# Dilated q, k and v in seven products: one encoder layer on one Trainium2 core

## The chip, the cores and the metric

The program runs on one core of a Trainium2 chip. Five engines work side by side: TensorE (PE in the profile; PEld is its weight load), VectorE (DVE), ScalarE (ACT), GpSimd (POOL) and SyncE (SP), which issues most DMAs. The metric is the time of one execution on the device, in microseconds; shorter is better. Of the kernel before, three executions took 1961.05, 1961.09 and 1961.69 us; their median, 1961.09 us, is the time to compare with.

## The reference

One layer of a bidirectional encoder on 256 tokens of width 4096, all in float32:

```python
h = rms_norm(x, g_mix)
proj = h @ w_in                       # 4096 x 9792
c_q, c_kv, k_rope, gate_a, q_b, k_b, v_b, gate_b = split(proj)   # 1024|512|64|2048|2048|2048|2048|2048
q_a  = rms_norm(c_q) @ w_uq           # 1024 x 3072, rotary on 64 of each head's 192
kv   = rms_norm(c_kv) @ w_ukv         # 512 x 4096
y_a  = rms_norm(mla_attention(...)) * silu(gate_a)               # group A: 16 heads of 128
y_b  = rms_norm(dilated_mixture_attention(q_b, k_b, v_b)) * silu(gate_b)   # group B: 16 heads of 128
x = x + concat([y_a, y_b]) @ w_out    # 4096 x 4096
x = x + (p @ w_ple) * sigmoid(rms_norm(x, g_ple) @ w_ple_gate)   # 256 x 4096 and 4096 x 4096
out = rms_norm(x, g_final)
```

The dilated attention of group B merges three patterns (window, dilation) by their softmax denominators; with 256 tokens that is one softmax over the 256 x 256 scores of a head, with a distance penalty and a table of how many patterns hold each pair. `g_ple` is scaled by 3.513, nothing else is changed in the inputs.

## The kernel before

**The products.** Every operand of a large product is split into two float32r halves, `hi` (a rounded copy, made by ACT, L115) and `lo` (the rest, a subtraction on DVE, L116), and a product is three matmuls: `hi*hi`, `lo*hi`, `hi*lo` (`mm`, L130 to L135). A weight is fetched by SP into one of 4 `raw` buffers of 512 KB, converted to `hi` and `lo` in a ring of 3 buffers (`wp`; some stages add more slots), and used by PE as the streamed operand, 512 columns at a time; the tokens' 128x128 blocks are the stationary operand.

**Two forms of a stage.** A `Chunk` computes 512 columns for both halves of the 256 tokens in two PSUM banks: a step takes two row blocks of 128 weights, and so 12 matmuls of 128x512. A `Block` (L691) computes 1024 columns in eight PSUM banks. Its row blocks go in pairs, by one of two recipes. In a plain pair two steps of 12 matmuls make eight products of 128 tokens x 128 rows x 512 columns. In a fast pair (`fast_steps`, L734) four steps make seven such products (M1 to M7), from four differences of weights that DVE forms (L742) and from four sums of token blocks that are made once for the whole stage (`add_sums`, L772); the seven are added up in PSUM over the pairs, and combined when the last pair is through: `..._mid` behind the last fast pair, `..._done` behind the last step of the block. The string in `mix` gives the order, C a plain pair and S a fast one.

**The order.** `steps` is the list of all steps in the order of PE: the four chunks of 400 columns with the latents, gate A's four chunks with the products of `w_uq` and `w_ukv` between them, then for each group of four dilated heads a chunk of q, of k and of v (`done_d`, L589), gate B's four chunks, three `Block`s and two chunks of `w_out`, three `Block`s and the rest of `w_ple_gate`. After each step `advance` (L240) is called once (a tick): it lets every small task go one `yield` further. Tasks are spawned by the `done` of a chunk (into `urgent`), or, for heads of attention, put into `waiting` and started one by one, two ticks apart, at most five at a time. So the engines' queues, which each execute in the order of the program, hold the conversions for the next steps and the pieces of small tasks in turn. A step's conversion stands two steps ahead of its use with the ring of 3, and five steps ahead where a stage has a longer ring (L1312).

**Attention.** A head (`attend`, L387) takes ten ticks: PE turns q and k (L393, L394), both are split (L397), PE makes the scores `s`, DVE and ACT the softmax (L420 to L433 in a dilated head), PE turns the weights (L440), they are split into `pt` (L443), PE multiplies with v into `o`, ACT copies it out (L449) and squares it (L451), POOL adds the squares (L453). The MLA heads run beside gate A's second chunk; the dilated heads of a group of four run beside the chunks of the next group, the last four beside gate B's first chunk. v comes split from `done_d`.

**Gates.** `done_gate` (L534) applies SiLU to a gate chunk, scales it, turns it on PE (L556), multiplies it with the attention output (L561), and splits the product into `yT`, the token side of `w_out`. The four chunks go in a chain, each behind the `yT` of the one before. `y_sums` makes the sums for the fast pairs of `w_out`.

**Banks.** PSUM has eight banks of 128x512, `m0` to `m3`, `s`, `o`, `t0`, `t1`. A stage's first matmul into a bank waits until the former contents have been read. In `w_out` the last chunk uses `o` and `m1` (L1128), and the first `Block` of `w_ple_gate` starts in `m1` (`TAGS`, L699).

## Time and profile before

The profiled execution took 1961.72 us, with a span of 1960.0 us on the core; the rest lies around the span.

| engine | busy, us | share of the span |
|---|---|---|
| PE (matmul) | 1941.6 | 99% |
| PEld (weight load) | 1658.0 | 85% |
| DVE | 1277.4 | 65% |
| ACT | 1011.1 | 52% |
| POOL | 71.2 | 4% |

HBM traffic is 188 GB/s over the span. A row of the profile's groups names line, engine, operation, out<-in with shapes, the count, then after a bar the busy time and the mean duration of one in ns, then the idle time before it and who ended it. A row of a table by stretches gives, after the bounds in us, the length, then for PE, PEld, DVE, ACT and POOL the busy time with the number of instructions that overlap the stretch, then PE's granted clock (1.00 is full), the share of the DMA engines and GB/s. In a timeline, a row is start, duration, engine, line, operation, with the idle time before it in brackets.

By stages, PE: the latents and gate A to about 441 us, the twelve chunks of dilated q, k and v with twelve of the sixteen dilated heads to about 1050, gate B to about 1226, `w_out` to about 1584, `w_ple_gate` to the end.

### The profile page before, as it was taken

What the parts mean: (1) busy time and instruction counts of PE and PEld (TensorE: products, weight loads), DVE (VectorE), ACT (ScalarE), POOL (GpSimd) and SP (SyncE); (2) the same over time, 40 slices, a digit from 0 to 9 for tenths busy, and PEclk for the clock granted to TensorE, in tenths of its full rate; (3) what the DMA queues carried; (4) which work ended last, traced back from release to release, by engine and by line L of the source; (5) the groups of instructions that cost most, each with busy time, mean ns of one, the idle gap of its engine ahead of it and who ended that gap; (6) DMA issues with size and microseconds to landing.
All of it is one profiled execution on the core that took longest, in us unless ns stands there. A gap on an engine that the chain in (4) does not pass through costs nothing.

```text
span 1960.0 us, 25219 instructions
## 1 busy us (share of the span) xinstructions
PE 1941.6 (99%) x9434; PEld 1658.0 (85%) x9434; DVE 1277.4 (65%) x1685; ACT 1011.1 (52%) x1375; POOL 71.2 (4%) x124
## 2 busy tenths in 40 slices
PE   9999999999999999999999999999999999999997
PEld 8998899988888888888888888888888878888887
DVE  7645566664564644645645555888867588888765
ACT  6544555554454544544544544555545455656543
POOL 1001111100000000000000100000000000000000
PEclk9999999999999999999999999999999999999999
DMA  7666544546656566566565666665656556566655
GB/s 251 189 185 198 167 145 141 155 151 204 184 182 194 161 192 190 157 193 186 167 194 179 219 187 200 198 208 194 204 185 208 189 188 213 195 223 197 227 186 177
DMA packets 175146, 370.56 MB, mean 189 GB/s; under 512 B 11924, under 2 KB 45808, under 8 KB 174768
## 3 DMA queue, kind: packets, MB, share of 16 engines
q1 hardware_dynamic: 173104, 361.80, 58.8%
q0 software_dynamic: 1920, 7.15, 1.0%
q8 instruction: 74, 1.21, 0.2%
q14 instruction: 48, 0.39, 0.1%
HBM read 364.72 MB, written 4.19 MB: 188 GB/s over the span
## 4 chain that ended last, share of the span: by engine, by line
PE 98%; DVE 1%; ACT 0%; DMA 0%; issue 0%; SPq 0%; DVEq 0%; ACTq 0%
PE m L133 26%; PE m L134 26%; PE m L135 26%; PE s L134 2%; PE s L135 2%; PE s L133 2%; PE t L133 2%; PE t L134 2%; PE t L135 2%; PE o L134 2%; PE o L135 2%; PE o L133 2%; PE t L440 1%; PE t L393 0%; DMA raw<-in_w_in_dram 0%; PE t L394 0%
## 5 line engine op out<-in xcount | busy, mean ns | idle before, releaser
L116 DVE TENSOR_TENSOR lo<-raw,hi 128x1024 fp32r<-128x1024 f32 (+4 forms) x596 | 695.2, 1171 | 534.9 <-ACT hi L115 534.4
L115 ACT ACTIVATE hi<-raw 128x1024 fp32r<-128x1024 f32 (+4 forms) x596 | 599.9, 1011 | 623.5 <-PE m L135 477.2
L133 PE MATMUL m<-hi,Ah 128*128 128x512 f32 (+2 forms) x1730 | 661.0, 382 | 2.7 <-ACT junk L672 1.8
L134 PE MATMUL m<-lo,Ah 128*128 128x512 f32 (+2 forms) x1730 | 655.0, 379 | 0.2 <-DVE lo L116 0.2
L135 PE MATMUL m<-hi,Al 128*128 128x512 f32 (+2 forms) x1727 | 653.4, 378 | 0.0
L133 PEld LDWEIGHTS m<-hi,Ah 128*128 128x128 f32 x1730 | 325.5, 188 | 55.8 <-issue 2.2
L135 PEld LDWEIGHTS m<-hi,Al 128*128 128x128 f32 x1727 | 324.7, 188 | 55.7 <-DVE Al L127 0.2
L134 PEld LDWEIGHTS m<-lo,Ah 128*128 128x128 f32 x1730 | 325.5, 188 | 52.8 <-DVE lo L116 0.5
L133 PE MATMUL m<-hi,B 128*128 128x512 f32 (+1 forms) x398 | 151.7, 381 | 0.0
L135 PE MATMUL m<-hi,B 128*128 128x512 f32 (+1 forms) x398 | 148.3, 373 | 0.0
L134 PE MATMUL m<-lo,B 128*128 128x512 f32 (+1 forms) x398 | 148.1, 372 | 0.0
L135 PEld LDWEIGHTS m<-hi,B 128*128 128x128 f32 x398 | 74.8, 188 | 10.8
L134 PEld LDWEIGHTS m<-lo,B 128*128 128x128 f32 x398 | 75.0, 188 | 9.7
L133 PEld LDWEIGHTS m<-hi,B 128*128 128x128 f32 x398 | 74.9, 188 | 9.8
L116 DVE TENSOR_TENSOR T<-t,T 128x512 fp32r<-128x512 f32 (+1 forms) x65 | 44.4, 683 | 39.4 <-ACT T L115 39.1
L453 POOL TENSOR_TENSOR acc<-acc,junk 128x256 f32<-128x256 f32 x30 | 29.3, 978 | 798.2 <-ACT junk L451 798.2
L116 DVE TENSOR_TENSOR B<-raw,B 128x1024 fp32r<-128x1024 f32 (+1 forms) x35 | 38.0, 1100 | 17.8 <-ACT B L115 17.8
L115 ACT ACTIVATE B<-raw 128x1024 fp32r<-128x1024 f32 (+1 forms) x35 | 32.8, 957 | 22.5 <-PE m L135 10.0
L133 PE MATMUL m<-B,Ah 128*128 128x512 f32 (+1 forms) x107 | 40.1, 374 | 0.0
L134 PE MATMUL m<-B,Ah 128*128 128x512 f32 (+1 forms) x107 | 40.0, 374 | 0.0
L135 PE MATMUL m<-B,Al 128*128 128x512 f32 (+1 forms) x107 | 40.0, 374 | 0.0
L115 ACT ACTIVATE T<-t 128x512 fp32r<-128x512 f32 (+1 forms) x65 | 38.3, 590 | 0.0
(625 smaller groups left out, 2427.6 us busy)
## 6 DMA issues: line engine op xcount, KB each, us to landing
raw<-in_w_in_dram SPq DMA_DIRECT2D x320, 512.0 KB, 3.4
raw<-in_w_out_dram SPq DMA_DIRECT2D x128, 512.0 KB, 4.5
raw<-in_w_ple_gate_dram SPq DMA_DIRECT2D x128, 512.0 KB, 4.6
raw<-in_w_in_dram SPq DMA_DIRECT2D x63, 400.0 KB, 3.3
raw<-in_w_uq_dram SPq DMA_DIRECT2D x32, 384.0 KB, 3.4
raw<-in_w_ukv_dram SPq DMA_DIRECT2D x16, 512.0 KB, 3.7
T<-in_x_dram POOLq DMA_DIRECT2D x8, 512.0 KB, 7.2
out_dram<-T SPq DMA_DIRECT2D x16, 256.0 KB, 2.6
```

Of the source, the lines that this page charges most:

```text
L115: nc.scalar.activation(hi, src, AF.Copy)
L116: nc.vector.tensor_tensor(lo, src, plain(hi), op=ALU.subtract)
L133: nc.tensor.matmul(ps, ah, bh, start=start, stop=False)
L134: nc.tensor.matmul(ps, ah, bl, start=False, stop=False)
L135: nc.tensor.matmul(ps, al, bh, start=False, stop=stop)
L440: nc.tensor.transpose(tp[:, k, t * P:(t + 1) * P], e[:, t, k * P:(k + 1) * P], ident)
L453: nc.gpsimd.tensor_tensor(acc, acc, sq, op=ALU.add)
```

## The change

Dilated q, k and v are no longer twelve chunks of 512 columns with four heads at a time, but six `Block`s of 1024 columns, in the order q, k, v of heads 0 to 7 and then of heads 8 to 15. Five of them have six fast pairs of sixteen and the last has four: 34 of 96 pairs. The sums of the token blocks for six pairs are made by a new task `x_sums`, beside gate A's last chunk; it waits for the MLA heads' statistics, which are now taken 32 steps earlier. `d_mid` and `d_done` combine the products and scale them by the tokens' norm.

All 16 dilated heads then wait until the last block is through and run beside the four chunks of gate B, one started two or three ticks behind the former. v is kept in float32, so a head splits its own part of v (`vs`) beside `pt`; its output is written over its q. The MLA half of the gated output stays in its place in float32 (`ya`), and `split_ya` splits it when the buffers of v and k are free. The chain of the gates follows the turned chunk now, not the split one.

`Block` gets its banks from outside. Consecutive blocks of q, k, v and of `w_out` alternate between two assignments, `EVEN` and `ODD`: a block begins with plain products (M2, X, M3, M4) in the four banks that the former block had for M1, M5, M6 and M7, the products that only fast pairs use and that `..._mid` reads out. The first block of `w_out` has four fast pairs instead of five. The last two chunks of `w_out` use `m2`, `m3` and `m0`, `m1`, and the blocks of `w_ple_gate` start in `m2`, `m3`, `s`, `o`.

```diff
     def advance():
         ticks[0] += 1
-        if waiting and len(running) < 5 and ticks[0] - ticks[1] >= 2 and waiting[0][0] <= flags:
+        if waiting and len(running) < 5 and ticks[0] - ticks[1] >= waiting[0][2] and waiting[0][0] <= flags:
             running.append(waiting.pop(0)[1])
             ticks[1] = ticks[0]
...
         pt = slot(f"T{2 + h % 2}", [2, NT, S], F32R)
         split(pt[:, 0], pt[:, 1], tp)
+        if dil:
+            vs = slot(("Q0", "T6")[h % 2], [2, NT, HD], F32R)
+            split(vs[:, 0], vs[:, 1], v)
+            v = lambda kt: (vs[:, 0, kt], vs[:, 1, kt])
         yield
         o = bank("o", [S])
         for k in range(NT):
-        nc.scalar.activation(y, o, AF.Copy)
+        nc.scalar.activation(y, by_token(o) if dil else o, AF.Copy)
...
+            u = slot(U_TAGS[dil][c], [NT, 512])
             for t in range(NT):
                 nc.scalar.activation(u[:, t], ps[t], AF.Tanh, scale=rxh[:, t:t + 1])
                 nc.vector.scalar_tensor_tensor(u[:, t], u[:, t], 1.0, ps[t], op0=ALU.add, op1=ALU.mult)
                 yield
-            while ("ry", dil) not in flags or (c and ("yT", dil, c - 1) not in flags):
+            while ("ry", dil) not in flags or (c and ("turned", dil, c - 1) not in flags):
                 yield
             yield
...
+                if b:
+                    flags.add(("turned", dil, c))
                 yield
...
-                    kt = 2 * b + k
-                    g = G["ob" if dil else "oa"][:, 4 * c + kt:4 * c + kt + 1]
-                    nc.vector.scalar_tensor_tensor(w[:, k], y[c // 2][:, 4 * (c % 2) + kt], g, tp[:, k],
+                    h = 4 * c + 2 * b + k
+                    g = G["ob" if dil else "oa"][:, h:h + 1]
+                    y = yb_rows(h) if dil else by_token(y_rows(ya, h))
+                    nc.vector.scalar_tensor_tensor(by_token(w[:, k]) if dil else y, y, g, by_token(tp[:, k]),
                                                    op0=ALU.mult, op1=ALU.mult)
+            if not dil:
+                flags.add(("gated", c))
+                return
+            while (("yT", 0, 3) if c == 0 else ("yT", 1, 1)) not in flags and c != 1:
+                yield
...
+    def split_ya():
+
+        for c, tag in enumerate(("B0", "B1", "B2", "B4")):
+            while not all(("head", 1, h) in flags for h in range(HEADS if c else HEADS // 2)):
+                yield
+            both = slot(tag, [2, 4, S], F32R)
+            yT[c] = [both[:, 0], both[:, 1]]
+            for b in range(2):
+                at = slice(4 * (c % 2) + 2 * b, 4 * (c % 2) + 2 * b + 2)
+                split(*(q[:, 2 * b:2 * b + 2] for q in yT[c]), ya[c // 2][:, at])
+                yield
+            flags.add(("yT", 0, c))
...
+    D_TAGS = {("q", 0): ("B5",), ("k", 0): ("B7a", "B7b"), ("v", 0): ("B0",),
+              ("q", 1): ("B6",), ("k", 1): ("B4",), ("v", 1): ("B1",)}
...
+    def d_mid(key, blk):
+        def task():
...
+            ps = blk.ps
+            sc = [(rxq if key[0] == "q" else rx)[:, t:t + 1] for t in range(NT)]
+
+            def add(h, t, m, old):
+                nc.vector.scalar_tensor_tensor(d[h][:, t], ps[m], sc[t], old, op0=ALU.mult, op1=ALU.add)
+
+            for t in range(NT):
+                nc.scalar.activation(d[0][:, t], ps["M1"], AF.Copy, scale=sc[t])
+            for t in range(NT):
+                add(1, t, "M6", d[0][:, t])
+            add(0, 1, "M7", d[1][:, 1])
+            add(1, 0, "M5", d[1][:, 0])
+            add(1, 1, "M5", d[0][:, 1])
+            flags.add(("mid", key))
+            yield
+        return task
...
+    def d_done(key, blk):
+        def task():
+            d = D[key]
+            sc = [(rxq if key[0] == "q" else rx)[:, t:t + 1] for t in range(NT)]
+            for m, t, h in (("M2", 0, 0), ("X", 1, 1), ("M3", 0, 1), ("M4", 1, 0)):
+                nc.vector.scalar_tensor_tensor(d[h][:, t], blk.ps[m], sc[t], d[h][:, t], op0=ALU.mult, op1=ALU.add)
+            if key == ("v", 1):
+                E["t"] = slot("T4", [2, NT, S])
+                for h in range(HEADS):
+                    waiting.append((set(), attend(
+                        h, lambda t, h=h: d_cols("q", h)[:, t], lambda t, h=h: d_cols("k", h)[:, t], None,
+                        d_cols("v", h), yb_rows(h), True), 2 + h % 2))
+                spawn(y_stats(1))
+                spawn(split_ya())
             yield
         return task
...
-        TAGS = dict(M1="m0", M2="m1", M3="m2", M4="m3", M5="s", M6="o", M7="t0", X="t1")
+        NAMES = "M2", "X", "M3", "M4", "M1", "M5", "M6", "M7"
+
+        def __init__(self, w, lhs, sums, name, order, needs, tags, tmp, ring):
             self.w, self.lhs, self.sums, self.name, self.needs, self.tmp = w, lhs, sums, name, needs, tmp
-            self.ring = ring
+            self.ring, self.tags = ring, dict(zip(self.NAMES, tags))
...
+                if isinstance(self.tmp, tuple):
+                    T.extend(slot(b, [2, Q]) for b in self.tmp)
+                else:
+                    both = slot(self.tmp, [4, Q])
+                    T.extend((both[:, :2], both[:, 2:]))
...
+        while not all(("yT", 0, c) in flags for c in range(FAST_O // 2)):
+            yield
+        yield from add_sums(FAST_O, lambda j: [q[:, 2 * (j % 2):2 * (j % 2) + 2] for q in yT[j // 2]], zy_dst, "Al1",
+                            "y_sums", y_s)
...
-    WIDE_PLE = {(0, 0): "m0", (0, 1): "s", (1, 0): "o", (1, 1): "t0"}
+    WIDE_PLE = {(0, 0): "m0", (0, 1): "m1", (1, 0): "t0", (1, 1): "t1"}
...
-    for g in range(4):
-        for i, off in enumerate((OFF_Q, OFF_K, OFF_V)):
-            add(from_x(off + 512 * g, 512, done_d(i, g)))
+    EVEN, ODD = ("m0", "m1", "s", "o", "m2", "m3", "t0", "t1"), ("m2", "m3", "t0", "t1", "m0", "m1", "s", "o")
+    LAST = "m2", "m3", "s", "o", "m0", "m1", "t0", "t1"
...
+    def x_sums():
+        while ("ry", 0) not in flags:
+            yield
+        yield from add_sums(6, lambda j: [q[:, 2 * (j % 4):2 * (j % 4) + 2] for q in xT[j // 4]],
+                            lambda j: slot(z_tags[j], [2, 4, P], F32R), "B0", "x_sums", x_s)
+
+    hook(64 + 16 + 64, lambda: spawn(y_stats(0)))
+    hook(64 + 16 + 64 + 12, lambda: spawn(x_sums()))
+    gated_rings = {("T4", "T7"): ("mid", ("k", 1)), "Al1": ("y_sums", FAST_O - 1)}
+    for n, key in enumerate((key, i) for i in range(2) for key in "qkv"):
+        off = {"q": OFF_Q, "k": OFF_K, "v": OFF_V}[key[0]] + 1024 * key[1]
+        order = mix("CCCCSCSCSCSCSCSC" if n < 5 else "CCCCCSCCSCCSCCSC")
+        ring = (["B4", "B6"], ["B4", "B6"], ["B4", "B6"], ["B4", "B1"], ["B1"], [("T4", "T7")])[n]
+        blk = Block(w_in[:, off:off + 1024], lhs_x, x_s, "x_sums", order, lambda kt: (), (EVEN, ODD)[n % 2],
+                    "B1" if n < 3 else ("T5", "T6"), WP + ring)
+        lay(blk, order, d_mid(key, blk), d_done(key, blk))
+    for c in range(4):
+        if c == 3:
+            hook(len(steps) + 8, lambda: spawn(y_sums()))
+        ch = from_x(OFF_GB + 512 * c, 512, done_gate(1, c))
+        ch.banks = M[c % 2]
+        add(ch)
+
     for k in range(WIDE_O):
-        hook(len(steps), only("t0", "m0"))
+        hook(len(steps), only(*(("t0", "t1"), ("m0", "m1"), ("m2", "m3"))[k]))
         for h in range(2):
             hook(len(steps) + 4 + h, lambda c=2 * k + h: load_res(c))
-        order = mix(("CCCCCSCSCSCSCSCC", "CCCSCSCSCSCSCSCC", "CCCSCCSCCSCCSCCC")[k])
+        order = mix(("CCCCCCSCSCSCSCCC", "CCCSCSCSCSCSCSCC", "CCCSCCSCCSCCSCCC")[k])
         blk = Block(w_out[:, 1024 * k:1024 * (k + 1)], lhs_y, y_s, "y_sums", order, lambda kt: need_y(kt // 2),
-                    "Al2" if k < 2 else "Al1", WP + (["Ah2", "Al1"] if k < 2 else [("T6", "T7")]))
+                    (EVEN, ODD)[k % 2], "Al2" if k < 2 else "Al1", WP + (["Ah2", "Al1"] if k < 2 else [("B7b", "T7")]))
         lay(blk, order, out_mid(k, blk), out_done(k, blk))
...
-        add(Chunk(cols(w_out, 512 * c, 512), 32, 512, lhs_y, ("m0", "s") if c == 6 else ("o", "m1"), done_o(c), need_y))
+        add(Chunk(cols(w_out, 512 * c, 512), 32, 512, lhs_y, ("m2", "m3") if c == 6 else ("m0", "m1"), done_o(c), need_y))
...
-                    lambda kt: [("x1T", kt // 4)], "B4", WP + ["B5", "B6"])
+                    lambda kt: [("x1T", kt // 4)], LAST, "B6", WP + ["B4", "B5"])
-    tail_banks = {6: (("m0", "s"), ("o", "t0")), 7: (("m1", "m3"), ("m2", "t1")), 8: (("m0", "s"), ("o", "t0"))}
+    tail_banks = {6: (("m0", "m1"), ("t0", "t1")), 7: (("m2", "o"), ("s", "m3")), 8: (("m0", "m1"), ("t0", "t1"))}
...
-        if i == 64 + 16 + 64 + 32:
-            spawn(y_stats(0))
-        if i == 64 + 16 + 64 + 32 + 192:
-            spawn(y_stats(1))
```

More of the change, by code (lines that the diff above doesn't have):

```diff
@@ L383, in encoder_layer @@
     ya = [None, None]
-    yb = [None, None]
     E = {}
@@ L532, in y_stats @@
         flags.add(("ry", dil))
+    U_TAGS = ("B7a", "B7b", "T5", "T6"), ("T7", "B7a", "B7b", "T4")
     def done_gate(dil, c):
         def task(ps):
-            y = (yb if dil else ya)
-            if not dil and c < 2:
-                u = slot(("B7a", "B7b")[c], [NT, 512])
-            else:
-                u = slot(f"T{5 + c % 2}", [NT, 512])
+            u = slot(U_TAGS[dil][c], [NT, 512])
             for t in range(NT):
@@ L960, in load_p @@
         split(pt[:, 0], pt[:, 1], tp, 0.5)
+        P4[0, 0] = slot("Q0", [Q])
+        P4[0, 1] = junk
         flags.add("pT")
@@ L1127, in encoder_layer @@
             hook(len(steps) + 11, lambda: spawn(load_p()))
[L1128 to L1129 removed]
+        add(Chunk(cols(w_out, 512 * c, 512), 32, 512, lhs_y, ("m2", "m3") if c == 6 else ("m0", "m1"), done_o(c), need_y))
+    kept = [("B1",), ("B4",), ("B5",), ("B6",), ("B7a", "T6")]
     stay = []
@@ L1234, in tiles @@
         n = at[0] % len(ring)
-        if ring[n] == "Al1" and ("y_sums", FAST_O - 1) not in flags:
+        if ring[n] in gated_rings and gated_rings[ring[n]] not in flags:
             n = 0
```

107 lines of the change are left out of this document (34 added, 73 removed).

## The prediction

> **What bounds the kernel now.** I read first the page's busy shares and its 40 slices, then the chain that ended last, then a table of busy time by stretches, then who PE waited for.
>
> ```profile
> span 1960.0 us, 25219 instructions
> ...
> PE 1941.6 (99%) x9434; PEld 1658.0 (85%) x9434; DVE 1277.4 (65%) x1685; ACT 1011.1 (52%) x1375; POOL 71.2 (4%) x124
> ...
> PEclk9999999999999999999999999999999999999999
> ...
> PE 98%; DVE 1%; ACT 0%; DMA 0%; issue 0%; SPq 0%; DVEq 0%; ACTq 0%
> ```
>
> PE is busy for 99% of the span and is 98% of the chain, at full clock in every slice. A busy PE can still be a waiting one, so the pace has to be read from the starts of matmuls. The next rows are from the timeline at the end of `w_out`.
>
> ```profile
> 1581.91 0.39 PE L133 MATMUL m<-hi,B7a 128*128 128x512 f32 x1
> ...
> 1583.72 0.39 PE L135 MATMUL m<-hi,B7b 128*128 128x512 f32 x1
> 1585.91 0.47 PE L133 MATMUL m<-hi,Ah 128*128 128x512 f32 x1 [1.80 <-ACT junk L672]
> ...
> 1582.75 1.21 DVE L116 TENSOR_TENSOR lo<-raw,hi 128x1024 fp32r<-128x1024 f32 x1
> 1583.88 0.68 DVE L116 TENSOR_TENSOR B<-B,B 128x512 fp32r<-128x512 f32 x1
> 1584.48 0.68 DVE L671 TENSOR_TENSOR T<-o,T 128x512 f32<-128x512 f32 x1
> 1585.08 0.68 DVE L671 TENSOR_TENSOR T<-m,T 128x512 f32<-128x512 f32 x1
> ...
> 1587.66 2.36 DVE L116 TENSOR_TENSOR B<-raw,B 128x1024 fp32r<-128x1024 f32 x2 [1.90 <-ACT B L115]
> ```
>
> From 1581.91 to 1583.72 there are eight pitches: 0.226 us for a matmul of 128x512, though each is shown 0.39 long. Then PE starts nothing for 2.19 us, 1.96 more than a pitch: the first product of the `w_ple_gate` block wants bank m1, and the last reader of m1's old contents is the second L671, which stands behind DVE's backlog and ends at 1585.76. The waits view knows one other stop of any size behind the start, (`o L133`, at 400 us), in a part that the change doesn't touch.
>
> ```profile
> PE m L133 <- ACT junk L672: 1.8, 1, 1.8
> ...
> PE o L133 <- ACT T L115: 0.7, 1, 0.7
> ```
>
> So the time is PE's instruction count times its pitch, as long as DVE and ACT keep up. How near they are to not keeping up is seen in stretches: plain chunks, the densest dilated attention, and the first `w_out` block, with fast pairs.
>
> ```profile
> core 0: us, PE busy (x) PEld busy (x) DVE busy (x) ACT busy (x) POOL busy (x), PEclk, DMA share, GB/s
> 690.00:735.00 45.00, 45.00 (x200) 37.29 (x199) 21.59 (x18) 17.74 (x18) 0.00 (x0) 1.00 0.64 197
> 654.00:668.00 14.00, 14.00 (x76) 12.10 (x75) 10.17 (x20) 9.29 (x18) 0.00 (x0) 1.00 0.49 151
> 1226.00:1313.00 87.00, 87.00 (x389) 72.04 (x388) 75.36 (x100) 50.23 (x56) 0.00 (x0) 1.00 0.60 199
> 1568.00:1617.00 49.00, 47.20 (x214) 38.75 (x213) 43.22 (x75) 27.43 (x36) 0.32 (x1) 1.00 0.58 188
> ```
>
> DVE is half idle under plain chunks, at 73% in dense attention, and at 87% in the `w_out` block, where PE still lost nothing. The last row is the stretch with the stop: 1.80 us less PE, and a granted clock of 1.00.
>
> **The change, part by part.**
>
> *Matmuls.* A fast pair has seven products where a plain one has eight, a product is three matmuls: 34 x 3 = 102 fewer. The first `w_out` block goes from five fast pairs to four: 3 more. In the order of instructions the built programs have 6906 and 6807 matmuls of 128x512, and equal numbers of all others. 99 x 0.226 = 22.4 us come off PE, the engine that bounds.
>
> *The stop at 1583.72.* The chunk before the `w_ple_gate` block now fills m0 and m1, and the block starts in m2, m3, s, o; m2 and m3 were read out a chunk earlier. The stop has no cause left: -1.96 us. Next late would be the third step's `B` conversion: its DVE half (1587.66, the first of two) is done by 1588.9, and without the stop PE gets there after two steps of 12, 1583.95 + 5.4 = 1589.4. It fits by 0.6, so I take -1.9; the ends are -1.9 and 0.
>
> *DVE and ACT in the six blocks.* Durations are from the groups kept apart by shape; L119 and L127 stand for operations out of PSUM, L778 for the short ones of the sums.
>
> ```profile
> L116 DVE TENSOR_TENSOR lo<-raw,hi 128x1024 fp32r<-128x1024 f32 x477 | 585.5, 1232 | 463.0 <-ACT hi L115 462.7
> L115 ACT ACTIVATE hi<-raw 128x1024 fp32r<-128x1024 f32 x477 | 503.1, 1060 | 546.1 <-PE m L135 416.2 <-PE s L135 57.1 <-issue 34.8
> L742 DVE TENSOR_TENSOR B<-raw,B 128x512 f32<-128x512 f32 x36 | 24.8, 689 | 0.6
> L116 DVE TENSOR_TENSOR T<-t,T 128x512 fp32r<-128x512 f32 x64 | 44.0, 688 | 39.4 <-ACT T L115 39.1
> L119 DVE SCALAR_TENSOR_TENSOR B<-m,st,B 128x512 fp32r<-128x512 f32 x8 | 5.7, 751 | 1.8 <-ACT B L118 1.8
> L127 DVE SCALAR_TENSOR_TENSOR Al<-t,gT,Ah 128x256 fp32r<-128x256 f32 x52 | 22.7, 478 | 2.3 <-ACT Ah L125 2.3
> L778 DVE TENSOR_TENSOR Al<-Al 128x128 f32<-128x128 f32 x9 | 2.3, 288 | 0.2
> ```
>
> A fast pair costs DVE 4 x 0.689 + 0.688 + 3 x 1.232 = 7.1 us, a plain pair 2 x 1.232 = 2.5. A block of ten plain and six fast pairs: 25 + 43 + nine read-outs x 0.751 = 6.8, together 74 us, against PE's (16 x 24 - 18) x 0.226 = 82.7: 90%, by means that overlap (1582.75 + 1.21 ends behind the next start, 1583.88). The `w_out` block carries 87% as measured, with the same recipe and without loss to PE; where S and C alternate, 7.1 + 2.5 = 9.6 stand under 4.7 + 5.4 = 10.1. ACT has 20 x 1.06 and 6 x 3.5 x 1.06, 43 of 82.7. I take 0 and keep 0 to +10 (0.3 us for each of 34 pairs).
>
> *Handing on the banks.* A new wait: a block's first products want the banks that `d_mid` of the former reads, one plain pair after the last fast one. The nearest case before is `wide_mid`, whose banks are wanted by the `w_ple` step, also one plain pair later.
>
> ```profile
> 1658.16 0.39 PE L135 MATMUL o<-hi,B7a 128*128 128x512 f32 x1
> ...
> 1659.06 0.68 DVE L922 TENSOR_TENSOR B<-B,o 128x512 f32<-128x512 f32 x1
> ...
> 1661.10 0.69 DVE L922 TENSOR_TENSOR B<-B,s 128x512 f32<-128x512 f32 x1
> ...
> 1665.19 0.39 PE L133 MATMUL s<-B,B 128*128 128x512 f32 x1
> ```
>
> M6 (`o`) is through at 1658.39 and the first add starts 0.67 behind it; the last of four ends at 1661.79, and its bank is used at 1665.19. `d_mid` has five adds of 0.751: 0.67 + 3.76 = 4.4 us behind M6, and M5's bank is wanted after M4 (0.68), a plain pair (5.43) and M2 (0.68), 6.8 us behind. Queued behind the waiting adds on DVE are the conversions from the fifth step on, which PE wants 10 us later. Margin 2.4 us: 0; the ends are 0 and 6 blocks x 1 us.
>
> *`x_sums` and the gates of group A* now fall into some 13 steps beside gate A's last chunk, 35 us of PE: six sums of 2 x 0.689 + 4 x 0.288 = 2.5 make 15 us, twelve gate products of 0.478 6, thirteen conversions 16: 37 us by means, of which the overlaps of some 50 starts (0.08 each) take 4, on a lead of two steps (5.4 us). 0 to +3; I take +0.5.
>
> *Sixteen heads beside gate B.* None of their work is new but the split of v (0.478 on DVE, as much on ACT), which was 2 x 0.751 for four heads; the cover is new. In the dense stretch before (654 to 668) a head starts every two steps, with DVE at 73% and no loss; now one starts every 2.5 steps, half a step (1.36 us) more of PE's time for 0.478 of v and half a conversion (0.62) more on DVE. So the heads are less crowded, but for some 15 x 2.5 + 10 = 47 steps on end. Behind them it is tightest: about 22 steps, 60 us of PE, with conversions 27, `y_sums` 15, `split_ya` and the splits of the gated product 14 x 0.688 = 9.6, and gate products 16 x 0.478 = 7.6, 59 us of DVE by means; the `w_out` block at its end lengthens its lead by three conversions, 3.7, that are not due at once. The stretch from 1226, 87% full, lost nothing; the backlog at 1583 cost 2. I take +1.5, ends 0 and +5. The split of v also stands between `pt` and the product with v, at one step's lead: 0 to 16 x 0.48 = 7.7; since a whole step (2.72) covers 0.688 + 0.478, 0.
>
> *DMAs.* SP issues the same bytes, in the 1024-column rows that `w_out` has, at 0.60 of the DMA engines in both cases; the distance table moves on POOL's queue to the last block's `d_mid`, six steps (16 us) ahead of its first reader, with nothing but the heads' squares behind it. 0.
>
> [...] In the quoted stretch with the 1.8 us stop the clock stayed at 1.00. [...]
>
> **Sum.** The profiled execution took 1961.7, 0.6 over the median of the runs. 1961.7 - 22.4 - 1.9 + 0.5 + 1.5 = 1939.4; less 0.6, 1938.8 us.
>
> **Rivals.**
>
> *Pile-ups at the two seams.* All of +3 and +5, and the stop at 1583 only half gone: 1938.8 + 6 + 1 = 1946. For it: DVE sums there are 37 us in 35 and 59 in 60 by means. Against: the lead of the conversions and a busy time that is less than the sum of means.
>
> [...]
>
> *DVE sets the pace of the fast pairs*, 5% over PE's 10.1 in each: 0.5 x 34 = +17, 1956. For it: 9.6 of 10.1. Against: 75 us in 87 with no loss.
>
> *Slower: the product with v.* With v's split in the link, PE waits in each dilated head for a whole chain of ACT and DVE behind L440: half of 1.06, 0.688 and 0.478, 1.7 us, 16 times, +27: 1966. It decides from 22.3 / 16 = 1.4 us a head. For it: the stop at 400 us is at this product. Against: that was one of 32 heads.
>
> **How the numbers follow.** The sum holds with 0.68 (by itself 1936 to 1942: no new wait at all, less the 0.6 by which the runs differ, or two and a half times my 2.0), pile-ups with 0.18, halved clock 0.02, DVE pace 0.06, slower 0.06. 0.2%, 3.9 us, is about what a measurement tells from no change. Of the last two cases 0.01 falls within 0.2% and 0.05 above it: faster 0.94. The range of 8 in 10 takes the sum's own and the pile-ups: 1936 to 1947.
>
> **What would show it.** Right: 128x512 matmuls at 0.226 in all six blocks, DVE at 80 to 90% there, no stop at the start of `w_ple_gate`, chain PE 98%. Wrong: PE waiting for `hi` or `lo` (L115, L116) in the blocks, for the read-outs at block ends, for `pt` and `vs` beside gate B, or for `y_sums` and `yT` at the start of `w_out`.

## The result, and the profile after

| | us, median | span of the profiled execution |
|---|---|---|
| before | 1961.07 | 1960.0 |
| after | 1947.72 (four runs, 1947.63 to 1949.53) | 1946.0 |

The ratio is 0.9934, with a 95% interval of 0.9916 to 0.9951. So 13.4 us were gained, where the prediction had 22.3; the time lies 0.7 us above its range. The profiled execution of after took 1947.77 us.

From the page of the kernel after: the span, the engines, the granted clock and the chain that ended last.

```profile
span 1946.0 us, 25440 instructions
...
PE 1924.3 (99%) x9335; PEld 1639.8 (84%) x9335; DVE 1448.3 (74%) x1973; ACT 1064.1 (55%) x1459; POOL 73.8 (4%) x124
...
PEclk9999999999999999999999999999999999999999
...
PE 96%; DVE 2%; ACT 1%; DMA 0%; issue 0%; SPq 0%; DVEq 0%; ACTq 0%
```

PE has 99 instructions fewer, 9335 for 9434. The chain is 96% PE, where it was 98%: DVE now has 2% of it and ACT 1%. Where they stand in it is seen by stretches. The bounds of the stages given for the kernel before are early at two places: gate A's last chunk is through by 494.9 us there (its first tanh, L542, starts then) and by 498.4 in after, and gate B's by 1237.1 and 1225.3. So the first row holds the end of gate A and the start of the first block, the second the rest of the six blocks of dilated q, k and v, the third gate B with all sixteen heads; then come the first `w_out` block and the start of `w_ple_gate`.

```profile
core 0: us, PE busy (x) PEld busy (x) DVE busy (x) ACT busy (x) POOL busy (x), PEclk, DMA share, GB/s
441.00:533.00 92.00, 92.00 (x424) 76.05 (x423) 70.33 (x113) 48.55 (x55) 0.00 (x0) 1.00 0.61 189
533.00:1000.00 467.00, 467.00 (x2062) 386.70 (x2061) 380.53 (x424) 247.33 (x257) 0.58 (x1) 1.00 0.63 202
1000.00:1226.00 226.00, 220.99 (x1118) 184.54 (x1117) 164.35 (x292) 137.21 (x238) 19.74 (x19) 0.99 0.51 160
1226.00:1313.00 87.00, 87.00 (x390) 71.93 (x389) 75.54 (x96) 49.32 (x57) 1.44 (x2) 1.00 0.66 218
1568.00:1617.00 49.00, 49.00 (x221) 40.42 (x220) 46.02 (x75) 29.01 (x36) 0.00 (x0) 1.00 0.62 199
```

PE is full in every stretch but the third. There DVE is busy for 164.35 of 226 us, 73%, less than in the blocks (81%) and in `w_out` (87%), where PE is busy throughout. Who PE waited for in the whole of after:

```profile
PE s L134 <- DVE T L116: 2.8, 6, 1.0
PE s L133 <- ACT T L115: 2.0, 2, 1.3
...
PE o L133 <- ACT T L115: 0.7, 1, 0.7
PE m L133 <- ACT Ah L125: 0.4, 1, 0.4
PE o L134 <- DVE T L116: 0.3, 1, 0.3
```

The stop of 1.8 us at the start of `w_ple_gate` is gone, and the scores (`s`) wait for the split of the turned q and k. The rows of `o` are one MLA head's at 403 us, and before has the same.

The waits view leaves out what is hidden inside a busy PE. So I took, from the starts of all matmuls, each distance to the next, less the usual one for these two shapes (0.226 us between two of 512 columns, 0.117 between two of 256), and added up what is over, in us. Below it is called lost time. A nanosecond more or less in the usual distance would move the sum from 1000 to 1226 us by about 1 us, in every kernel alike, so differences between kernels count, not the sums.

| stretch | before | after |
|---|---|---|
| to 441 us | 10.4 | 10.7 |
| end of gate A, dilated q, k, v and gate B, to 1226 us | 6.8 | 17.2: to 1000 us 1.5, gate B from 1000 us 15.7 |
| `w_out`, `w_ple_gate` | 6.4 | 4.3 |

That is 8.6 us more in all; with 99 x 0.226 = 22.4 us of matmuls gone it makes -13.8, and the spans differ by 14.0. So the gain is there, and some 9 us of it were given back at one place: the sixteen heads beside gate B. There the first six heads, to 1060 us, lose 2.0 us; from 1060 to 1150 it is 11.5.

### The profile page after: what moved, and what is told of

Same layout as the page of the kernel before. It is cut to its first block, busy times and chain, and to the rows that moved or that the text cites. A ratio compares the mean times of both kernels' runs of the same rounds, so it can differ in the third digit from the quotient of the medians.

```text
span 1946.0 us, 25440 instructions
## 1 busy us (share of the span) xinstructions
PE 1924.3 (99%) x9335; PEld 1639.8 (84%) x9335; DVE 1448.3 (74%) x1973; ACT 1064.1 (55%) x1459; POOL 73.8 (4%) x124
## 4 chain that ended last, share of the span: by engine, by line
PE 96%; DVE 2%; ACT 1%; DMA 0%; issue 0%; SPq 0%; DVEq 0%; ACTq 0%
PE m L133 21%; PE m L134 21%; PE m L135 21%; PE t L133 4%; PE t L134 4%; PE t L135 4%; PE o L134 3%; PE o L135 3%; PE o L133 3%; PE s L134 3%; PE s L135 3%; PE s L133 3%; PE t L440 1%; DVE lo L116 0%; ACT hi L115 0%; DMA raw<-in_w_in_dram 0%
## 5 line engine op out<-in xcount | busy, mean ns | idle before, releaser
L116 DVE TENSOR_TENSOR lo<-raw,hi 128x1024 fp32r<-128x1024 f32 (+3 forms) x507 | 570.8, 1134 | 308.1 <-ACT hi L115 307.1
L115 ACT ACTIVATE hi<-raw 128x1024 fp32r<-128x1024 f32 (+3 forms) x507 | 496.6, 986 | 388.2 <-PE m L135 200.5
L133 PE MATMUL m<-hi,Ah 128*128 128x512 f32 (+2 forms) x1203 | 459.5, 382 | 0.4 <-ACT Ah L125 0.4
L134 PE MATMUL m<-lo,Ah 128*128 128x512 f32 (+2 forms) x1203 | 452.2, 376 | 0.2 <-DVE lo L116 0.2
L135 PE MATMUL m<-hi,Al 128*128 128x512 f32 (+2 forms) x1199 | 450.4, 376 | 0.0
L135 PEld LDWEIGHTS m<-hi,Al 128*128 128x128 f32 x1199 | 225.7, 188 | 36.5 <-DVE Al L127 0.2
L134 PEld LDWEIGHTS m<-lo,Ah 128*128 128x128 f32 x1203 | 226.9, 189 | 33.1 <-DVE lo L116 0.5
L133 PEld LDWEIGHTS m<-hi,Ah 128*128 128x128 f32 x1203 | 226.7, 188 | 33.3 <-ACT Ah L125 0.7
L116 DVE TENSOR_TENSOR B<-raw,B 128x1024 fp32r<-128x1024 f32 (+1 forms) x81 | 87.1, 1088 | 30.4 <-ACT B L115 30.4
L133 PE MATMUL m<-B,Ah 128*128 128x512 f32 (+1 forms) x184 | 68.2, 371 | 0.0
L134 PE MATMUL m<-B,Ah 128*128 128x512 f32 (+1 forms) x184 | 68.2, 371 | 0.0
```

The lines of the kernel that those rows point to most:

```text
L115: nc.scalar.activation(hi, src, AF.Copy)
L116: nc.vector.tensor_tensor(lo, src, plain(hi), op=ALU.subtract)
L133: nc.tensor.matmul(ps, ah, bh, start=start, stop=False)
L134: nc.tensor.matmul(ps, ah, bl, start=False, stop=False)
L135: nc.tensor.matmul(ps, al, bh, start=False, stop=stop)
```

## The experiments

Two kinds of loss must be kept apart. In both kernels the second large matmul behind a run of 128x128 transposes comes 0.09 us late, 38 times from 441 us to 1226 before and 38 times in 1000 to 1226 after: 3.5 us that belong to the transposes of heads and gates and are not new. The other 12 come from waits, and the runs below ask for their cause. Of these 12 us, 1.4 are matmuls at half clock behind the longest wait (last section). Of the runs below that change after, only the one with the youngest head first and the two with both links lengthened have such a stretch near gate B in their profiles (granted clock over the span 0.997, 0.996 and 0.996); in the others up to 1.4 us of a smaller sum may be the clock alone. In the expectations A (the link) says that the one step between the split of the turned q and k and the scores is too short, B (the load) that DVE and ACT fall behind, so that a wait moves elsewhere when one link is lengthened, C that the splits of v are the cause. Lost time is of 1000 to 1226 us where nothing else is said.

**One link, or its neighbours.** A tick more between that split and the scores:

```diff
             flags.add(("read", h))
+            yield
         yield
         s = bank("s", [NT, S])
```

> The changed kernel with one more tick in each dilated head, between the split of the turned q and k (L397) and the scores. In the changed kernel's trace PE loses 15.8 us against its own pitch between 1000 and 1226 us, 8 of them where the first score products (s<-T, L133 to L135) wait for that split. Theory A (the link): the split has one step of lead and stands in the queues behind another head's softmax (L420, L422, L424), so with two ticks these waits go, and the half clock behind the longest of them (1.4 us) with them: 1939 to 1941 us. Theory B (the load): DVE and ACT are too full for 47 steps on end, wherever it shows; the waits move to other products, and the time stays at 1946 or above.

Measured: 1946.1 us, lost 13.9. The scores no longer wait. Who PE waits for in this kernel, 1000 to 1232 us:

```profile
PE t L393 <- DVE T L116: 5.2, 4, 1.5
```

Now the next head's transposes of q and k wait, for the bank that the same late split still reads. A's time, 1941 at most, was missed, and B's wait that moves elsewhere came.

Without the splits of v in heads 2 to 15 (they multiply with those of heads 0 and 1, so the output is another):

```diff
-            vs = slot(("Q0", "T6")[h % 2], [2, NT, HD], F32R)
-            split(vs[:, 0], vs[:, 1], v)
+            if h < 2:
+                E["vs", h] = slot(("Q0", "T6")[h], [2, NT, HD], F32R)
+                split(E["vs", h][:, 0], E["vs", h][:, 1], v)
+            vs = E["vs", h % 2]
```

> The changed kernel in which heads 2 to 15 do not split their own v: they use the split v of heads 0 and 1, so 14 splits (an ACT and a DVE operation of 128x256) are left out. Theory C (the split of v, my rival for a slower result): it is the cause, and most of the 15.8 us of waits beside gate B go: 1940 or below. Theory A (the link between the split of q and k and the scores): the backlog in front of that link is shorter by 0.4 us in each head, which takes 2 to 4 us: 1943.5 to 1946. Theory B (the load): 10% of the heads' work less, 4 to 8 us: 1940 to 1944.

Measured: 1943.67 us, lost 12.1, 3.6 less. C, 1940 or below, falls as the whole cause; A and B both allowed this time.

All heads three ticks apart:

```diff
-                        d_cols("v", h), yb_rows(h), True), 2 + h % 2))
+                        d_cols("v", h), yb_rows(h), True), 3))
```

> The changed kernel with dilated heads started three ticks apart, instead of two and three in turn. Theory A (the link): with three ticks the split of q and k of one head never falls into the tick of another head's softmax (L420 to L424), so the waits at the scores go; the last head ends some 7 steps later, 19 us, which takes slack from the sums at the start of w_out: 1940 to 1944. Theory B (the load): a sixth less work in a step, the waits fall by a part: 1942 to 1946. If the late end costs more than the waits: above 1948.

Measured: 1950.34 us, lost 15.2, and 2.4 more from 1226 on, where a gate's transposes behind the later heads wait; the expectation had a time above 1948 for such a late end. In 12 smaller waits the scores lose 7.2 us, for 7.7 in after, where A had said that three ticks would take these waits away.

The tasks of a tick youngest head first instead of oldest first, while dilated heads run:

```diff
-            for task in list(pool):
+            for task in list(pool)[::-1 if pool is running and D else 1]:
```

> The changed kernel in which, from the dilated heads on, the heads in flight are advanced youngest first in a tick instead of oldest first; nothing else changes. The split of q and k then stands in front of another head's softmax in the queues of ACT and DVE. Theory A (the link): the waits at the scores go, and some may come up at the product with v, which then stands behind younger heads: 1939 to 1944. Theory B (the load): the order doesn't matter, 1946 to 1949.

Measured: 1953.59 us, lost 21.8: the products with v (9.9) and the transposes of the weights (5.6) now wait. The same work in another order costs 6 us more, which neither A nor B had: order matters, and not only the amount.

Only the split of q and k first in its tick, the rest oldest first:

```diff
-            for task in list(pool):
+            for task in sorted(pool, key=lambda q: pool is running and ages.get(q) != 1 if D else 0):
+                ages[task] = ages.get(task, 0) + 1
```

> The changed kernel in which, among the dilated heads in flight, the one whose next piece is the split of its turned q and k is advanced first in a tick; the others stay oldest first. Theory A, as the runs so far leave it: the waits are at whatever wants that split first (the scores in the changed kernel; with one more tick before the scores it was the turning bank that the split still read), because the split is queued last in its tick, behind a softmax, on both ACT and DVE. In front, it is done within the step: the waits at s<-T go, no new ones of their size come up, 1938.5 to 1942. Theory B (load, wherever it shows): 1945 or above.

Measured: 1945.41 us, B's number, lost 13.3, of which the product with v has 5.9. The same with v split three ticks earlier, beside L427:

```diff
                 nc.vector.scalar_tensor_tensor(e[:, t], e[:, t], 1.0, E["d"][:, 1, t], op0=ALU.mult,
                                                op1=ALU.mult, accum_out=l[:, t:t + 1])
+            vs = slot(("Q0", "T6")[h % 2], [2, NT, HD], F32R)
+            split(vs[:, 0], vs[:, 1], v)
+            v = lambda kt: (vs[:, 0, kt], vs[:, 1, kt])
         yield
```

> The same, and the split of v moves from the tick of the split of pt, one tick before the product with v, to the tick of the second softmax product (L427), four ticks before it. Theory A: the split of v no longer lengthens a link of one step; 0.5 to 2 us below the run with the order alone. Theory B: no difference between the two.

Measured: 1945.49 us, no different, as B had it; lost 13.5. And the split of q and k first with both links lengthened by a tick: the `yield` of the first experiment, and one more before the product with v:

```diff
             v = lambda kt: (vs[:, 0, kt], vs[:, 1, kt])
+            yield
         yield
         o = bank("o", [S])
```

> The changed kernel with three edits together: a young head's split of turned q and k goes first in its step, and both links that had one step (that split to the scores, the split of the turned weights and of v to the product with v) get two. Waits in gate B's chunks (1000 to 1226 us) were 15.7 us; single edits moved them (13.3 to 14.0). Theory A, every link of one step is too short, and a wait only goes when all of them are lengthened: waits of 6 to 9 us there, 1938.5 to 1941.5 us. Theory B, DVE and ACT serve these stages late by more than a step now and then, whatever the lead: waits move on again, 1944 us or more.

Measured: 1950.34 us, lost 13.3, and 9.1 from 1226 on for after's 4.3. Scores and products with v no longer wait; PE waits at two other links, the transposes of the attention weights, one step behind their scaling, and a gate's transposes (here 1000 to 1232 us):

```profile
PE t L443 <- ACT T L436: 3.5, 6, 2.0
PE t L565 <- DVE B7b L573: 3.0, 1, 3.0
```

So no single link is at fault (A falls, B holds): with the waits taken from some links, others have them. Heads two ticks apart (`2` for `2 + h % 2`), again without 14 splits of v:

> The changed kernel with the dilated heads two ticks apart, as before the change, and without 14 of the 16 splits of v (heads 2 to 15 use the split v of heads 0 and 1, so this part of the computation is left out): the head's work of the kernel before, but sixteen in a row. If the row of sixteen is what brings the waits (in groups of four they were 0.25 us a head), the excess between 1000 and 1230 us is above the 12.1 us that 2.5 ticks without those splits left, and the time is above 1944. If the pattern of two and three ticks brought them, the excess falls to about 4 + 4 us: 1939 to 1941.

Measured, in one execution: 1943.5 us, lost 12.0, as with two and three in turn without these splits (1943.67 and 12.1): the spacing isn't the cause.

**Load or order.** DVE's subtraction of the weights' low parts left out in gate B (the high parts are used twice, so part of the products is missing):

```diff
-                split(hi[:, k], lo[:, k], r[:, k])
+                if ch.light:
+                    nc.scalar.activation(hi[:, k], r[:, k], AF.Copy)
+                else:
+                    split(hi[:, k], lo[:, k], r[:, k])
...
-                       (hi[:, k], lo[:, k]),
+                       (hi[:, k], hi[:, k] if ch.light else lo[:, k]),
```

> A load test: the changed kernel without DVE's subtraction of the low parts of the weights in the four gate B chunks (64 instructions of 1.23 us; the matmuls run on the high parts twice, so that part of the computation is left out). Waits were 15.7 us in these chunks, 3.5 of them the short waits for the low parts themselves. Theory B, DVE's queue is what makes the heads' stages late: waits of 1 to 5 us, 1934 to 1938 us. Theory A, the links are short whatever DVE's load, since each passes ACT and DVE in turn: only the 3.5 us and a little go, 1941 to 1944 us.

Measured: 1938.86 us, lost 7.4, of which 3.5 are the 0.09 us behind transposes, which stay: they are no waits for low parts, for which the expectation took them. The other lost time goes from 12.2 to 3.9 us. The time lies between the two theories, 0.9 us above B's and 2 below A's. That speaks for DVE, but it takes away two things at once: 1.23 us of DVE a step, and a place where DVE stands still. The next rows, of the timeline of after, show such a place; three dots stand for rows left out.

```profile
1094.60 0.28 PE L135 MATMUL s<-T 128*128 128x256 f32 x1
...
1095.05 0.27 PE L394 MATMUL t<-ident,B 128*128 128x128 f32 x1
...
1095.54 0.15 DVE L430 RECIPROCAL st<-st 128x2 f32<-128x2 f32 x1
...
1095.73 0.91 ACT L433 ACTIVATE T<-T,st 128x256 f32<-128x256 f32 x2 [2.51 <-DVE st L430]
...
1096.54 1.04 ACT L115 ACTIVATE hi<-raw 128x1024 fp32r<-128x1024 f32 x1
...
1097.62 1.22 DVE L116 TENSOR_TENSOR lo<-raw,hi 128x1024 fp32r<-128x1024 f32 x1 [1.92 <-ACT hi L115]
...
1098.76 0.68 DVE L420 SCALAR_TENSOR_TENSOR T<-T,s 128x512 f32<-128x512 f32 x1
...
1099.47 0.69 DVE L422 TENSOR_REDUCE st<-T 128x2 f32<-128x512 f32 x1
...
1100.26 0.91 ACT L424 ACTIVATE T<-T,st 128x256 f32<-128x256 f32 x2 [2.67 <-DVE st L422]
...
1101.07 0.58 ACT L115 ACTIVATE T<-t 128x512 fp32r<-128x512 f32 x1
...
1101.68 0.69 DVE L116 TENSOR_TENSOR T<-t,T 128x512 fp32r<-128x512 f32 x1 [1.52 <-ACT T L115]
...
1102.43 0.39 PE L134 MATMUL s<-T 128*128 128x256 f32 x1 [0.31 <-DVE T L116]
```

The scores are through at 1094.88, and their reader L420 starts only at 1098.76, though DVE is idle from 1095.7 to 1097.6: in DVE's queue it stands behind the subtraction `lo`, which stands for 1.92 us until ACT has made `hi`; ACT was late with it because L433 ahead of it had waited 2.51 us for DVE. Then ACT stands 2.67 us for DVE's L422, with the split of the next head's q and k behind it, which were turned at 1095.3; then DVE stands 1.52 us for ACT's half of that split, and then PE 0.31 us for DVE's. Each queue waits for the other, in order, while DVE is idle for 27% of these 226 us and ACT for 39%.

The theories from here on: L, DVE is too full; O, the two queues wait for each other in order. The test leaves the work and takes one of these waits away: a subtraction goes into DVE's queue one step behind ACT's copy (the step's matmuls follow two steps behind that copy, so one step of lead is left). `light` marks gate B's chunks.

```diff
-                split(hi[:, k], lo[:, k], r[:, k])
+                if ch.light:
+                    nc.scalar.activation(hi[:, k], r[:, k], AF.Copy)
+                    late.append(lambda hi=hi, lo=lo, r=r: nc.vector.tensor_tensor(lo, r, plain(hi), op=ALU.subtract))
+                else:
+                    split(hi[:, k], lo[:, k], r[:, k])
...
     def convert(upto):
+        while late:
+            late.pop(0)()
+            held[0] -= 1
```

> The changed kernel with one edit in the four gate B chunks: DVE's subtraction for the low part of a step's weights is put into its queue one step later than ACT's copy that it needs (it is needed two steps after that). DVE does the same 64 subtractions, but no longer stands at one of them, with the heads' instructions queued behind it, until ACT has come to the copy. Theory L, DVE is simply too full: no difference, 1946.5 to 1949 us, 14 to 17 us of waits in 1000 to 1226 us. Theory O, the two queues wait for each other in order: waits of 7 to 11 us there, 1939 to 1943 us.

Measured: 1940.99 us (1940.94 to 1941.23), ratio to before 0.9894 (0.9877 to 0.9910), lost 8.8. O holds, and L falls: of the 8.3 us of lost time that leaving out the subtraction had brought, moving it in the queue brings 6.9, with no work left out. Neither profile has the 1.4 us at half clock; without these it is 5.5 of 6.9. What DVE waited for from 1000 to 1226 us, in after and then in this kernel:

```profile
DVE lo L116 <- ACT hi L115: 48.8, 39, 2.0
DVE T L116 <- ACT T L115: 10.6, 7, 1.5
```

```profile
DVE T L117 <- ACT T L116: 30.6, 26, 2.7
...
DVE lo L1268 <- ACT hi L1267: 4.2, 5, 1.5
```

And ACT's waits for DVE's row maxima and reciprocals, after and then this kernel:

```profile
ACT T L433 <- DVE st L430: 32.6, 16, 2.6
ACT T L424 <- DVE st L422: 27.2, 16, 2.7
```

```profile
ACT T L425 <- DVE st L423: 13.3, 16, 2.1
ACT T L434 <- DVE st L431: 12.9, 12, 1.7
```

DVE's waits for `hi` fall from 48.8 to 4.2 us and ACT's two waits for DVE from 59.8 to 26.2, with DVE's busy share at 74% for 73%. DVE still waits for ACT, but now at the splits of the heads' own tiles (`T`, 30.6 us for 10.6): what changed is less how long it stands than at which instruction, and what is queued behind that. The stretch from 1000 to 1226 us in this kernel:

```profile
1000.00:1226.00 226.00, 224.94 (x1149) 189.06 (x1148) 168.28 (x304) 144.25 (x244) 15.87 (x19) 1.00 0.55 166
```

The control, the same late subtraction in the kernel before, in its sixteen chunks:

> The control: the kernel before with the late subtraction of the weights' low parts in its sixteen chunks of dilated q, k, v and gate B (441 to 1226 us, where its own waits are 6.8 us in all). Theory O, the coupling of the two queues costs time only where many heads follow each other: 0 to 3 us less, 1958.5 to 1961.5 us. If it gains 6 us here too, the late subtraction helps any chunk, and the row of sixteen heads isn't what the changed kernel paid for.

Measured: 1961.15 us beside 1961.65, ratio 0.9999 (0.9989 to 1.0008); lost from 441 to 1226 us 6.8, as without it. In the kernel before DVE waited for `hi` there too (441 to 1226 us), and PE paid nothing for it:

```profile
DVE lo L116 <- ACT hi L115: 324.6, 250, 2.2
```

So an engine's wait says little until one sees who stands behind it, and for how long.

The splits of v once more (left out in 14 heads), with the late subtraction:

> The changed kernel with the late subtraction (1941.0 us, 8.8 us of waits in 1000 to 1226 us) and without 14 of the 16 splits of v (heads use those of the first two, so that part of the computation is left out). Without the late subtraction these splits cost 4 us. Theory O: they cost it by lengthening the chain that the weights' subtraction waits behind, so nearly nothing is left of it, 1940 to 1941 us. Theory L, they cost it by their time on DVE: 1936.5 to 1938.5 us.

Measured: 1940.09 us, 0.9 less; lost in gate B 8.8, unchanged. So of the 4 us that these splits cost in after, nearly all came from the two queues' waits for each other.

**Combinations.** POOL makes the low part of v, with the split first and both links lengthened:

```diff
-            split(vs[:, 0], vs[:, 1], v)
+            nc.scalar.activation(vs[:, 0], v, AF.Copy)
+            nc.gpsimd.tensor_tensor(vs[:, 1], v, plain(vs[:, 0]), op=ALU.subtract)
```

> As the kernel with both links lengthened, and POOL instead of DVE subtracts the low part of v (16 instructions of 0.42 us on DVE). Theory A: within 1 us of the kernel with both links lengthened. Theory B, DVE's load counts: 1 to 2 us faster than that. If POOL is slow at it, its result comes late and the product with v waits: slower.

Measured: 1945.39 us (1943.57 to 1946.65), 5 less than without POOL and more than B allowed for a load of 0.42 us a head. Lost 12.3, only 1.0 less; from 1226 on 3.6 less, as the stop of 3.0 us at a gate's transposes now falls at 1224.2, ahead of that bound. POOL with v split early:

> As the kernel with a young head's split first and v split three steps earlier (1945.5 us, 13.5 us of waits), and POOL instead of DVE makes the low part of v (0.9 us on POOL in the run before, 0.42 on DVE). Theory L: DVE's load falls by 0.17 us a step and the waits by 2 to 4 us, 1941.5 to 1943.5 us. Theory O: POOL's subtraction is one more thing that DVE does not queue behind, but the weights' low parts remain: 0 to 2 us, 1943.5 to 1945.5 us.

Measured: 1946.41 us, 0.9 more than without POOL, lost 14.7: neither theory's number. Less load on DVE didn't help here, which is against L, but in the run before it did; why the two differ isn't settled. With the late subtraction, the split first and v early, then all with POOL:

> The late subtraction of the weights' low parts together with a young head's split first in its step and v split three steps earlier. Theory O: the best of these orders, waits of 5 to 9 us in 1000 to 1226 us, 1937.5 to 1941 us. Theory L: as without the late subtraction, 1944.5 to 1946.5 us.

> All edits of the last three together (late subtraction of the weights' low parts, split of q and k first, v three steps earlier, its low part by POOL). Both theories: the fastest, 1937 to 1941 us under O, 1941.5 to 1943.5 us under L. That it is slower than each alone would speak for POOL's result being late.

Measured: 1941.62 and 1941.91 us, lost 9.7 and 10.0. No wait for `s` or `o` is left in the waits view, but PE waits for low parts made late (2.3 and 2.1 us). So these edits don't add up, O's ranges are missed by under 1 us, and none of the versions that do all the work was measured faster than the late subtraction alone.

**Where it begins.** The task of gate B's first chunk held back by eight ticks:

```diff
+            for _ in range(8 if (dil, c) == (1, 0) else 0):
+                yield
             u = slot(U_TAGS[dil][c], [NT, 512])
```

> The changed kernel with the SiLU task of gate B's first chunk held back by eight ticks (some 28 us). In the changed kernel the first six heads, to 1060 us, have 2.0 us of waits in 60 us, and from the seventh, where the first chunk's tanh and product also fall, 11.5 us in 90 us. If the gate's work on top of the heads starts the waits, 1060 to 1090 us loses less than 2 us (4.6 in the changed kernel) and the stop moves to about 1087 to 1092. If the seventh head in a row is enough, the stop at 1062.7 stays and 1060 to 1090 us loses 3.5 us or more. The time is 1945 to 1949 us in both cases.

Measured: 1947.53 us, lost 15.3. From 1060 to 1090 us 2.9 (4.6 in after), from 1090 to 1120 4.1 (2.9). That is between the two cases, but 1.4 of after's 4.6 us are at half clock, and without these 3.2 stand against 2.9. The wait of 1.31 us at the seventh head's scores is gone and the one of 0.34 behind it stays; later heads wait more. So the gate's work made the longest stop, and waits begin at the seventh head without it. How long a row of heads must be to get there isn't settled.

**The banks by themselves.** The kernel before with the banks of the last two `w_out` chunks exchanged, so that bank m1 is free early:

```diff
-        ("m0", "s") if c == 6 else ("o", "m1"), done_o(c)
+        ("o", "m1") if c == 6 else ("m0", "s"), done_o(c)
```

> The kernel before with one edit: the last two chunks of w_out exchange their banks, so that the last one ends in m0 and s, and the first block of w_ple_gate finds m1 read out. My step for this stop: the 1.96 us at 1583.7 us go, and the next conversion is in time: 1959.1. The other reading (a backlog on DVE is next): above 1960.5.

Measured: 1959.62 us beside 1961.28 (ratio 0.9990, 0.9981 to 0.9999); lost from 1226 us on 4.2 for 6.4. The stop goes with the bank; the interval only just leaves out no gain at all.

## Why the prediction was wrong

*Matmuls, -22.4.* Right: 99 fewer, 0.226 us each.

*The stop at 1583.72, -1.9.* Right: -2.1 of lost time in after, -2.2 by itself in the kernel before (1.7 of time).

*DVE and ACT in the six blocks, 0.* Right: from 490 to 1000 us 0.5 us were lost, with DVE at 81% (the means had made 90%).

*Handing on the banks, 0.* Right: from 441 to 1000 us the waits view has no row at all.

*`x_sums`, +0.5.* Inside its ends. The sums start at 458 us. From 441 to 490 us 1.0 was lost, and nearly nothing there in the kernel before; about half of it lies behind six runs of gate A's transposes.

*Sixteen heads beside gate B, +1.5, ends 0 and +5.* This step failed: 15.7 us lost for the 6.8 that before lost over all its chunks with the same heads, +8.9. The step priced the heads by DVE's load, from a stretch with DVE at 73% and no loss, found "the heads are less crowded", and looked for trouble behind them. The load was as said, 73%; behind them PE was busy for 87.00 of 87 us. What the step left out is that a late instruction holds up its queue, and that the two queues here depend on each other several times a head, most links with one step's lead. The quoted dense stretch had those waits as well (DVE 1.99 us for `hi`, 1.52 for a head's split), but its heads came in fours.

*The clock, 0.* That it would stay full was the author's estimate; in the kernel before only the one stop of 1.8 us, which left it at 1.00, spoke for it. It fell to half behind waits of 1.31 and 0.34 us, for 1.4 of the 8.9 us.

*The split of v in the link, 0, ends 0 and 7.7.* That "a whole step (2.72) covers 0.688 + 0.478" compared durations alone. Leaving 14 of the splits out brought 3.6 us of lost time, up to 1.4 of it by the clock, and none with the late subtraction: their price is their place in the queues. At the product with v of the dilated heads the waits view has no row.

Of the rivals, the halved clock, 0.02, came in part: no run shows the 4.1 us that it put behind one long stop at a seam; after has no stop at a seam, and its half clock was in gate B and cost 1.4 us. Pile-ups at the two seams, 1946, came near the time but had the place wrong: neither seam piled up and the stop went. The product with v, at 1.7 us a head, was the right kind of mechanism at the wrong link, and three times too dear with 27 us: the scores, earlier in the head, have 7.7 of the lost time. Of the 2.2 us of the predicted gain that the late subtraction still lacks (1940.99 against 1938.8), 1.5 lie between 441 and 1226 us: 10.3 are lost there, 3.5 more than in the kernel before, and the prediction had 2.0 for `x_sums` and the heads.

## What to carry to other kernels

An engine at 73% can still be late for what the next engine needs, if its queue holds an instruction that waits for another engine which in turn waits for it: price a row of small dependent tasks by the waits in each queue and what stands behind them, not by the busy share. Putting the dependent half of a conversion one step later into its queue, when it isn't needed yet, gave 6.7 us here, of a loss that sixteen heads had brought, with no work left out; lengthening single links only moved the wait. Heads in fours cost nearly nothing here (in the kernel before, the waits view has no row of PE from 441 to 1226 us), which didn't show what sixteen in a row cost.

## What was not expected of the hardware

PE ran at half clock behind two waits of 1.31 and 0.34 us. Matmul starts of after around the first stop, and the granted clock (the column behind POOL) by stretches of 2 us:

```profile
1061.03 0.39 PE L135 MATMUL m<-hi,Al 128*128 128x512 f32 x1
1062.73 0.39 PE L133 MATMUL s<-T 128*128 128x256 f32 x1 [1.31 <-ACT T L115]
1063.45 0.38 PE L134 MATMUL s<-T 128*128 128x256 f32 x1 [0.34 <-DVE T L116]
```

```profile
1062.00:1064.00 2.00, 0.94 (x5) 0.74 (x6) 1.04 (x2) 2.00 (x5) 0.00 (x0) 1.00 0.14 52
1064.00:1066.00 2.00, 2.00 (x9) 1.63 (x8) 2.00 (x4) 1.90 (x4) 1.17 (x1) 0.66 0.08 7
1066.00:1068.00 2.00, 2.00 (x7) 1.52 (x6) 2.00 (x7) 0.25 (x1) 0.00 (x0) 0.50 0.76 254
1068.00:1070.00 2.00, 2.00 (x15) 1.88 (x14) 0.98 (x2) 1.54 (x5) 0.00 (x0) 0.98 0.60 165
```

The two waits, 0.7 us apart, were followed by seven matmuls at 0.427 us instead of 0.226, 1.4 us more. In the run with both links lengthened and v split by DVE, single stops of 2.0 us (at 1118.7) and 3.0 (at 1227.9) each had some 3.4 us at a granted clock of 0.50 behind them; the mean is 0.98 from 1040 to 1150 us, around the first of them, and 0.996 over the span. In the first experiment, stops of up to 1.5 us left it at 1.00 (0.998 over the span, as in the kernel before), and so did the single stop of 1.8 us in the kernel before, at 1583.72 (1.00 in each 2 us from 1582 to 1590). What decides isn't settled by these runs.
